# Projecting a memory's K and V straight into transposed form, on eight cores of one chip

## The chip, the cores and the metric

One Trainium2 chip, eight cores. Each core runs the same program on its own prompt sequence (2048 tokens) and its own 16 sample tokens. The metric is the device time of the slowest core, in microseconds (us).

Engine names in the profile: PE is TensorE (PEld its weight loads), DVE is VectorE, ACT is ScalarE, POOL is GpSimd, SP is SyncE, which here issues the loads of x and every store of an output. A PSUM bank is one of the eight buffers of 128 x 512 float32 (PS in the kernel) that its matmuls write to. Half clock means a stretch in which the profile's clock records grant TensorE 0.5 of its full speed. Filler is work that is queued in between other work, to be done where PE would otherwise wait.

## The reference, cut to what matters

```python
def mem_kv(mem, g_mem, w_kv):                       # once per layer
    kv = jnp.einsum('bnd,de->bne', rmsnorm(mem, g_mem), w_kv)
    k, v = jnp.split(kv, 2, axis=-1)                # both are outputs as well
    return k.reshape(b, n, 4, 256), v.reshape(b, n, 4, 256)

def mem_attend(u, k, v, w_q, w_o):
    q = einsum('btd,de->bte', u, w_q)               # heads of 256
    p = softmax(einsum('bthd,bnhd->bhtn', q, k) / 16)
    return einsum('btd,de->bte', einsum('bhtn,bnhd->bthd', p, v), w_o)
```

There are 256 memory tokens and 1024 channels, two layers, so four projections of 256 x 1024 by 1024 x 1024 per core. K and V have to be delivered (float32) and are used inside.

## The kernel before

The kernel doesn't attend with K and V as such. It folds K into the query weights (`wqk = wq . K^T`) and V into the output weights (`vwo = V . wo`), once per layer. Both folds, as the kernel writes them, take K and V with channels on the partitions. Before the change they were projected with tokens on the partitions, copied out, stored, and then turned by matmuls with an identity:

```python
# cut: indices, slices and views that don't matter here
def rows(name, od, nb, half):          # layer 0; 4 calls per tensor
    bk = nxt()                         # next PSUM bank
    for kc in range(NCH):              # 8 matmuls of 512 columns
        mm(PSv(bk, 0, 512), MEMN(kc, sl(nb*128, (nb+1)*128)), Wt(kc, hs), kc == 0, kc == NCH-1)
    cp(ST[i](), PSv(bk, 0, 512), eng=ACT)          # float32, for the store
    cp(NB(nb, hs), ST[i](), eng=DVE)               # bfloat16
    dma(SP, DV(od[0, nb*128:(nb+1)*128, hs]), ST[i](), f"rst{i}")

def turn(nb, half):                    # 4 calls per tensor
    for j in range(4):                 # 4 matmuls of 128 columns with the identity
        mm(PSv(bk, j*128, (j+1)*128), NB(nb, sl(c*128, (c+1)*128)), IDB(), True, True)
    cp(TR(...), PSr(bk, ...), eng=evac_eng())      # ScalarE and VectorE in turn

def foldk(dc):                         # 2 x 4 matmuls of 256 columns, 2 copies
    ...
```

These pieces are filler between other work. The parts of the schedule that matter here:

```python
# prelude: software pipeline over 16 blocks of x; step s does
#   stB(s-1): pool bands, stC(s-2): transposes of x block s-2, stA(s+1): statistics, then extra[s]
for i, a in enumerate(quad): extra[12 + i].append(lambda a=a: rows("wk0", mk_d, *a))
for i, a in enumerate(quad): extra[16 + i // 2].append(lambda a=a: turn(*a))
extra[11].append(lambda: norm_a(0, BUF[0], parts=2))    # ScalarE: squares, 2 x 1664 columns
extra[12].append(lambda: norm_r(0, BUF[0], RSTDE))      # PE: sums the squares, after rows(0)
for i in range(4):                                      # VectorE: 2 multiplications per step
    extra[13 + i].append(lambda i=i: norm_s(0, R_ATTN, BUF[0], RSTDE, cs=(2*i, 2*i+1)))
...
wq_turn(0)                             # turn wq, fold K: 8 x (8 matmuls of 128, 8 of 256)
for dc in range(NCH):
    if dc + 1 < NCH: wq_turn(dc + 1)
    foldk(dc)
    if dc == 0: samples_a()            # VectorE: 1.27 us multiplication, 0.68 us cast
# stC(15) ends with last_rows(): a 1.28 us VectorE multiplication, then the load of the V weights
late = rows(V) x4, turn(V) x4, foldv x8   # popped one or two per score chunk of the first two tiles
# layer 1: the same pieces, as fill in layer 0's MLP; the conv stage stands between that and layer 1's attention
```

The softmax here doesn't subtract the row's maximum and nothing guards it: scores larger than these inputs give would overflow.

## Time and profile before

| | before |
|---|---|
| time of the slowest core, median of the first 3 runs | 1623.22 us (1622.68 to 1623.79) |
| span of the profiled run, slowest core / fastest core | 1624.3 / 1618.2 us |
| PE, VectorE, ScalarE busy | 97%, 53%, 35% |

From the page of the kernel before, the busy time by engine (us, share of the span, instructions), and below it the shares of the chain of work that ended last:

```profile
PE 1575.0 (97%) x10104; PEld 906.3 (56%) x10104; DVE 854.2 (53%) x1907; ACT 560.8 (35%) x1054; POOL 113.9 (7%) x245
...
PE 92%; DVE 2%; ACT 2%; DMA 2%; issue 2%; POOL 0%; DVEq 0%; ACTq 0%; SPq 0%; POOLq 0%
```

PE is the bound, at 97% of the span and 92% of the chain, so I count work taken from VectorE (53%) or ScalarE (35%) only where PE waits for it. The groups of the kernel before by form show the matmuls concerned (line, engine, operation, out and in, shapes, count, then busy us, mean ns of one, idle us before them and what ended it). L292 is the line of the matmul helper:

```profile
L292 PE MATMUL PS<-MEM 128*128 128x512 bf16 x192 | 47.1, 383 | 0.0
...
L292 PE MATMUL PS<-MEM 128*128 128x256 bf16 x128 | 18.6, 294 | 2.1 <-DVE MEM L345 1.9 <-ACT MEM L343 0.2
...
L292 PE MATMUL PS<-MEM 128*128 128x128 bf16 x192 | 15.2, 227 | 1.2 <-DVE MEM L327 1.2
```

128 of the 192 matmuls of 512 columns are the projections and 64 of the 192 of 128 columns the transposes. The mean length of one record at 512 columns (383 ns) is more than the time from its start to the next one's start, so the records overlap. I take the time from start to start as a matmul's cost: in the traces 215.8 ns at 512 columns, 109.1 at 256, 55.8 at 128, at the full granted clock.

The waits view of the kernel before, PE alone, from 64 to 160 us (who waited for whom: us in total, times, longest):

```profile
PE PS L296 <- DVE MEM L339: 3.1, 1, 3.1
PE PS L292 <- DVE MEM L345: 2.7, 2, 1.9
PE PS L292 <- ACT MEM L343: 0.2, 1, 0.2
```

L345 is VectorE's copy, L343 ScalarE's. The 2.7 us are 1.87 us at the fold of K (ending at 93.6 us) and 0.84 us in the fold of V (about 149 us). The 3.1 us are the late x blocks at 64 us. VectorE is nearly full in the stretch of the K fold, as the windows view of the kernel before shows (busy us of each engine from 86 to 95 us, granted clock, DMA share, GB/s):

```profile
86.00:95.00 9.00, 6.94 (x90) 6.01 (x87) 8.33 (x14) 5.54 (x12) 0.90 (x1) 0.93 0.12 39
```

The engines stand in the order PE, PEld, DVE, ACT, POOL: VectorE is busy for 8.33 of 9 us on this core (5), and the granted clock was 0.93 in the mean.

### The profile page before, as it was taken

What the parts mean: (1) busy time and instruction counts of PE and PEld (TensorE: products, weight loads), DVE (VectorE), ACT (ScalarE), POOL (GpSimd) and SP (SyncE); (2) the same over time, 40 slices, a digit from 0 to 9 for tenths busy, and PEclk for the clock granted to TensorE, in tenths of its full rate; (3) what the DMA queues carried; (4) which work ended last, traced back from release to release, by engine and by line L of the source; (5) the groups of instructions that cost most, each with busy time, mean ns of one, the idle gap of its engine ahead of it and who ended that gap; (6) DMA issues with size and microseconds to landing.
All of it is one profiled execution on the core that took longest, in us unless ns stands there. A gap on an engine that the chain in (4) does not pass through costs nothing.

```text
span 1624.3 us, 28431 instructions; the slowest of 8 cores (1618.2 to 1624.3 us)
## 1 busy us (share of the span) xinstructions
PE 1575.0 (97%) x10104; PEld 906.3 (56%) x10104; DVE 854.2 (53%) x1907; ACT 560.8 (35%) x1054; POOL 113.9 (7%) x245
## 2 busy tenths in 40 slices
PE   4899999999999999999999999999999999999997
PEld 3775555555555556555555555555555555555565
DVE  5666675655444444445666665766455444442235
ACT  4756344541122222222133224433643112213453
POOL 2002121110000000000000001121010000000000
PEclk8899999999999999999999999999999999999999
DMA  9978793575537516066000009694654663000012
GB/s 228 208 116 156 161 183 68 122 148 77 85 66 126 107 24 105 1 104 109 1 1 1 1 1 151 130 201 96 126 118 68 101 105 52 14 1 1 40 64 108
DMA packets 84565, 145.13 MB, mean 89 GB/s; under 512 B 4286, under 2 KB 37310, under 8 KB 84412
## 3 DMA queue, kind: packets, MB, share of 16 engines
q0 software_dynamic: 67568, 84.08, 35.4%
q1 hardware_dynamic: 16860, 59.24, 10.6%
q8 instruction: 84, 1.38, 0.3%
q14 instruction: 53, 0.43, 0.1%
HBM read 212.42 MB, written 14.36 MB: 140 GB/s over the span
## 4 chain that ended last, share of the span: by engine, by line
PE 92%; DVE 2%; ACT 2%; DMA 2%; issue 2%; POOL 0%; DVEq 0%; ACTq 0%; SPq 0%; POOLq 0%
PE PS L292 89%; PE PS L296 2%; DVE MEM L327 1%; ACT MEM L319 1%; PE PS L301 1%; DMA MEM<-gv 1%; DMA MEM<-x 1%; ACT MEM L308 1%; DVE MEM L331 0%; DVE MEM L345 0%; DVE MEM L339 0%; POOL MEM L354 0%; ACT MEM L343 0%; DVEq L1389 0%; ACTq L1389 0%
## 5 line engine op out<-in xcount | busy, mean ns | idle before, releaser
L292 PE MATMUL PS<-MEM 128*128 128x416 bf16 (+7 forms) x9024 | 1501.3, 327 | 8.3 <-DVE MEM L345 2.7
L292 PEld LDWEIGHTS PS<-MEM 128*128 128x128 bf16 (+1 forms) x9024 | 837.3, 98 | 659.8 <-issue 38.5
L319 ACT ACTIVATE MEM<-PS 128x416 f32<-128x416 f32 (+5 forms) x469 | 238.9, 510 | 632.5 <-PE PS L292 622.7
L331 DVE TENSOR_TENSOR MEM<-PS,MEM 128x416 f32<-128x416 f32 (+6 forms) x533 | 297.8, 575 | 264.2 <-PE PS L292 256.1
L331 DVE TENSOR_TENSOR MEM<-MEM 128x416 bf16<-128x416 f32 (+3 forms) x282 | 159.9, 584 | 198.8 <-ACT MEM L319 189.5
L327 DVE SCALAR_TENSOR_TENSOR MEM<-MEM 128x416 bf16<-128x416 f32 (+7 forms) x322 | 176.9, 601 | 126.9 <-ACT MEM L319 108.5
L319 ACT ACTIVATE MEM<-MEM 128x416 bf16<-128x416 f32 (+9 forms) x299 | 185.2, 631 | 146.5 <-DVE MEM L331 111.6
L304 DVE SCALAR_TENSOR_TENSOR MEM<-MEM,PS 128x256 f32<-128x256 f32 x256 | 105.2, 420 | 72.0 <-PE PS L292 49.0
L343 ACT COPY MEM<-PS 128x512 f32<-128x512 f32 (+3 forms) x73 | 39.2, 536 | 129.5 <-PE PS L292 119.1
L296 PE MATMUL PS<-MEM 128*128 128x128 bf16 (+4 forms) x896 | 61.0, 248 | 16.3 <-DVE MEM L339 9.4
L296 PEld LDWEIGHTS PS<-MEM 128*128 128x128 bf16 (+2 forms) x896 | 49.2, 107 | 30.2 <-issue 28.6
L343 ACT CAST MEM<-PS 128x512 bf16<-128x512 f32 (+2 forms) x65 | 35.2, 554 | 68.0 <-PE PS L292 67.3
L345 DVE CAST MEM<-PS 128x512 bf16<-128x512 f32 (+1 forms) x76 | 48.5, 658 | 11.7 <-PE PS L292 11.7
L354 POOL DMA_DIRECT2D MEM<-cv x64 | 47.7, 745 | 13.4 <-PE PS L292 13.4
L319 ACT ACTIVATE PS<-PS 128x416 f32<-128x416 f32 (+3 forms) x67 | 33.2, 495 | 41.5 <-PE PS L292 41.1
L327 DVE SCALAR_TENSOR_TENSOR MEM<-PS,MEM 128x1024 f32<-128x1024 f32 (+1 forms) x17 | 21.8, 1283 | 44.1 <-ACT MEM L319 44.1
L301 PE MATMUL PS<-MEM 128*128 128x128 f32 (+5 forms) x184 | 25.0, 277 | 18.3 <-DMA MEM<-gv 8.4
L351 POOL MEMSET MEM<- 128x4 bf16 (+1 forms) x96 | 15.0, 159 | 359.1 <-PE PS L296 298.5
L301 PEld LDWEIGHTS PS<-MEM 128*128 128x128 f32 (+5 forms) x184 | 20.9, 146 | 21.4 <-issue 19.9
L339 DVE TENSOR_SCALAR MEM<-MEM 128x1024 bf16<-128x1024 f32 (+1 forms) x18 | 17.9, 997 | 24.0 <-ACT MEM L319 24.0
L354 POOL DMA_DIRECT2D MEM<-w_up x36 | 20.6, 582 | 132.5 <-PE PS L292 132.5
L354 POOL DMA_DIRECT2D MEM<-w_down x22 | 13.8, 635 | 202.2 <-PE PS L292 158.1
(28 smaller groups left out, 137.3 us busy)
## 6 DMA issues: line engine op xcount, KB each, us to landing
MEM<-ck SPq DMA_DIRECT2D x64, 512.0 KB, 6.2
MEM<-cv POOLq DMA_DIRECT2D x64, 256.0 KB, 5.8
MEM<-w_down POOLq DMA_DIRECT2D x6, 2048.0 KB, 17.7
MEM<-x SPq DMA_DIRECT2D x16, 512.0 KB, 14.2
MEM<-w_kv POOLq DMA_DIRECT2D x4, 2048.0 KB, 17.9
MEM<-w_o POOLq DMA_DIRECT2D x4, 2048.0 KB, 22.7
MEM<-w_up POOLq DMA_DIRECT2D x32, 256.0 KB, 13.0
MEM<-w_up POOLq DMA_DIRECT2D x4, 2048.0 KB, 17.1
```

The source lines that it names most:

```text
L292: P.add(PE, "c", lambda e, o=out.ap, l=lhsT.ap, r=rhs.ap: e.matmul(out=o, lhsT=l, rhs=r, start=start, stop=stop), [lhsT, rhs], [out])
L296: P.add(PE, "c", lambda e, o=out.ap, l=lhsT.ap, r=rhs.ap: e.matmul(out=o, lhsT=l, rhs=r, start=start, stop=stop, is_transpose=is_transpose ...
L301: P.add(PE, "c", lambda e, o=out.ap, i=in_.ap, d=ident.ap: e.transpose(out=o, in_=i, identity=d), [in_, ident], [out])
L304: P.add(DVE, "c", lambda e, o=out.ap, a=in0.ap, b=in1.ap, c=acc.ap: e.scalar_tensor_tensor(out=o, in0=a, scalar=1.0, in1=b, op0=ALU.mult, ...
L308: P.add(ACT, "c", lambda e, o=out.ap, i=in_.ap, a=acc.ap: e.activation(out=o, in_=i, func=AF.Square, accum_out=a), [in_], [out, acc])
L319: P.add(ACT, "c", lambda e, o=out.ap, i=in_.ap: e.activation(out=o, in_=i, func=func, bias=bias, scale=sc), rd, [out])
L327: P.add(eng, "c", lambda e, o=out.ap, a=in0.ap, b=in1.ap: e.scalar_tensor_tensor(out=o, in0=a, scalar=sc, in1=b, op0=op0, op1=op1), rd, [out])
L331: P.add(eng, "c", lambda e, o=out.ap, a=in0.ap, b=in1.ap: e.tensor_tensor(out=o, in0=a, in1=b, op=op), [in0, in1], [out])
L339: P.add(eng, "c", lambda e, o=out.ap, a=in0.ap: e.tensor_scalar(out=o, in0=a, scalar1=sc, scalar2=None, op0=op0), rd, [out])
L343: P.add(ACT, "c", lambda e, o=out.ap, i=in_.ap: e.copy(out=o, in_=i), [in_], [out])
L345: P.add(eng, "c", lambda e, o=out.ap, i=in_.ap: e.tensor_copy(out=o, in_=i), [in_], [out])
L354: return P.add(q, "d", lambda e, o=out.ap, i=in_.ap: e.dma_start(out=o, in_=i), [in_], [out], chan=chan, after=after)
```

## The change

Intent: swap the operands of the projection. Each matmul now loads a 128 x 128 block of the weights (LDWEIGHTS 128x128 in the trace) and takes the 256 normalised memory tokens as its 256 columns; K and V come out with channels on the partitions, as the folds take them. The transposes, their copies and a bfloat16 buffer go; the outputs are stored as [1024, 256] per layer, and the host lays them out (that time is not in the metric).

```diff
-    mk_d = dout("mk", [2, NMEM, D])            # mv alike
+    mk_d = dout("mk", [2, D, NMEM])
+    def project(Wt, memn, dst, st, od, k, chan):       # 4 calls per tensor
+        bk = nxt()
+        for j in range(2):
+            c = 2 * k + j
+            for kc in range(NCH):                      # 2 x 8 matmuls of 256 columns
+                mm(PSv(bk, j*NMEM, (j+1)*NMEM), Wt(kc, sl(c*128, (c+1)*128)), memn(kc), kc == 0, kc == NCH-1)
+        cp(st(), PSv(bk, 0, 2*NMEM), eng=ACT)
+        cp(dst, ..., eng=DVE)
+        dma(SP, DV(od[2*k*128:(2*k+2)*128, :].rearrange("(j p) n -> p j n", p=128)), ..., chan)
-        for i, a in enumerate(quad): extra[12 + i].append(lambda a=a: rows("wk0", mk_d, *a))
-        for i, a in enumerate(quad): extra[16 + i // 2].append(lambda a=a: turn(*a))
+        for k in range(4): extra[13 + k].append(lambda k=k: kv("wk0", mk_d, k))     # kv calls project
-        late.extend(rows("wv0") x4); late.extend(turn x4)
+        late.extend(kv("wv0") x4)
-                    for _ in range(1 if k == 0 or m > 3 else 2): late.pop(0)()
+                    late.pop(0)()
     # (rows and turn deleted in both layers, layer 1's fill list rebuilt with the same spacing,
     #  host: mk and mv transposed; all cut here)
```

Layer 0's K projections now stand at steps 13 to 16 of the prelude instead of 12 to 15.

More of the change, by code (lines that the diff above doesn't have):

```diff
@@ L165, in build_program @@
     ncp_d = dout("ncp", [2, D])
-    mk_d = dout("mk", [2, NMEM, D])
-    mv_d = dout("mv", [2, NMEM, D])
+    mk_d = dout("mk", [2, D, NMEM])
+    mv_d = dout("mv", [2, D, NMEM])
     nps_d = dout("nps", [NS, 15, D])
@@ L449, in build_program @@
     late = []
+    def project(Wt, memn, dst, st, od, k, chan):
[3 more added lines that the diff above has]
+            for kc in range(NCH):
+                mm(PSv(bk, j * NMEM, (j + 1) * NMEM), Wt(kc, sl(c * 128, (c + 1) * 128)), memn(kc), kc == 0, kc == NCH - 1)
+        cp(st(), PSv(bk, 0, 2 * NMEM), eng=ACT)
+        cp(dst, V(st.ap.rearrange("p (j n) -> p j n", j=2), st().ivs), eng=DVE)
+        dma(SP, DV(od[2 * k * 128:(2 * k + 2) * 128, :].rearrange("(j p) n -> p j n", p=128)),
+            V(st.ap.rearrange("p (j n) -> p j n", j=2), st().ivs), chan)
     def prelude():
@@ L454, in prelude @@
         MEMN = su.alloc(BF16, [NCH, NMEM])
-        NB = su.alloc(BF16, [2, D])
+        SQJ = su.alloc(BF16, [D])
         TR = su.alloc(BF16, [NCH, NMEM])
@@ L592, in mem_stats @@
             for nb in range(2):
-                sumsq(NB(nb), MR[nb](), st_(0, 16 + nb))
+                sumsq(SQJ(), MR[nb](), st_(0, 16 + nb))
                 rstd(16 + nb)
@@ L614, in prelude, with kv @@
         st_ctr = [0]
-        def rows(name, od, nb, half):
-            bk = nxt()
+        def kv(name, od, k):
             i = st_ctr[0] % 3
             st_ctr[0] += 1
-            hs = sl(half * 512, (half + 1) * 512)
-            Wt = W(name)
-            for kc in range(NCH):
-                mm(PSv(bk, 0, 512), MEMN(kc, sl(nb * 128, (nb + 1) * 128)), Wt(kc, hs), kc == 0, kc == NCH - 1)
-            cp(ST[i](), PSv(bk, 0, 512), eng=ACT)
-            cp(NB(nb, hs), ST[i](), eng=DVE)
-            dma(SP, DV(od[0, nb * 128:(nb + 1) * 128, hs]), ST[i](), f"rst{i}")
-        def turn(nb, half):
-            bk = nxt()
-            for j in range(4):
-                c = half * 4 + j
-                mm(PSv(bk, j * 128, (j + 1) * 128), NB(nb, sl(c * 128, (c + 1) * 128)), IDB(), True, True)
-            cp(TR(sl(half * 4, half * 4 + 4), sl(nb * 128, (nb + 1) * 128)), PSr(bk, "p (j t) -> p j t", j=4), eng=evac_eng())
+            project(W(name), MEMN, TR(sl(2 * k, 2 * k + 2)), ST[i], od[0], k, f"rst{i}")
         def wq_turn(dc):
@@ L695, in samples_c @@
             dma(POOL, SO(), DV(wsrc_sq(wsrc["wo0"])), f"w{slot_of['wo0']}")
-        quad = [(nb, half) for nb in range(2) for half in range(2)]
         extra = {s: [] for s in range(20)}
@@ L704, in prelude @@
         extra[7] = [poolws]
-        for i, a in enumerate(quad):
-            extra[12 + i].append(lambda a=a: rows("wk0", mk_d, *a))
-        for i, a in enumerate(quad):
-            extra[16 + i // 2].append(lambda a=a: turn(*a))
+        for k in range(4):
+            extra[13 + k].append(lambda k=k: kv("wk0", mk_d, k))
         extra[11].append(lambda: norm_a(0, BUF[0], parts=2))
@@ L735, in prelude @@
                 samples_c()
-        late.extend(lambda a=a: rows("wv0", mv_d, *a) for a in quad)
-        late.extend(lambda a=a: turn(*a) for a in quad)
+        late.extend(lambda k=k: kv("wv0", mv_d, k) for k in range(4))
         late.extend(lambda h=h, nb=nb: foldv(h, nb) for h in range(4) for nb in range(2))
@@ L758, in begin, with kv @@
             mem["n"] = s.alloc(BF16, [NCH, NMEM])
-            mem["st"] = [s.alloc(F32, [D]) for _ in range(2)]
-            mem["nb"] = s.alloc(BF16, [2, D])
+            mem["st"] = [s.alloc(F32, [512]) for _ in range(2)]
             n = mem["n"]
             dma(SP, V(n.ap.rearrange("p c n -> p (c n)"), n().ivs), DV(memn_d), "memn", after=tuple(spill))
-        def rows(name, od, nb, half):
-            bk = nxt()
-            st = mem["st"][nb]
-            hs = sl(half * 512, (half + 1) * 512)
-            Wt = W(name)
-            for kc in range(NCH):
-                mm(PSv(bk, 0, 512), mem["n"](kc, sl(nb * 128, (nb + 1) * 128)), Wt(kc, hs), kc == 0, kc == NCH - 1)
-            cp(st(hs), PSv(bk, 0, 512), eng=ACT)
-            cp(mem["nb"](nb, hs), st(hs), eng=DVE)
-            if half == 1:
-                dma(SP, DV(od[1, nb * 128:(nb + 1) * 128, :]), st(), f"kst{nb}")
-        def turn(dst, nb, half):
-            bk = nxt()
-            for j in range(4):
-                c = half * 4 + j
-                mm(PSv(bk, j * 128, (j + 1) * 128), mem["nb"](nb, sl(c * 128, (c + 1) * 128)), IDB(), True, True)
-            cp(dst[half](sl(0, 4), sl(nb * 128, (nb + 1) * 128)), PSr(bk, "p (j t) -> p j t", j=4), eng=evac_eng())
+        def kv(name, od, dst, k):
+            project(W(name), mem["n"], dst[k // 2](sl(k % 2 * 2, k % 2 * 2 + 2)), mem["st"][k % 2], od[1], k, f"kst{k % 2}")
         def foldk(dc):
@@ L807, in need_slot @@
             return fn
-        quad = [(nb, half) for nb in range(2) for half in range(2)]
         trk = [T(TRK.off + hf * 4 * NMEM * 2, BF16, [4, NMEM]) for hf in range(2)]
@@ L812, in kv1_fill @@
         items += [None] * 7
-        items += [lambda a=a: rows("wk1", mk_d, *a) for a in quad]
+        items += [lambda k=k: kv("wk1", mk_d, trk, k) for k in range(4)]
         items.append(lambda: swap("wk1", "wv1"))
-        items += [lambda a=a: turn(trk, *a) for a in quad]
+        items += [None] * 6
+        items += [lambda k=k: kv("wv1", mv_d, TRV, k) for k in range(4)]
+        items.append(lambda: swap("wv1", "wqT1"))
         items += [None] * 3
-        items += [lambda a=a: rows("wv1", mv_d, *a) for a in quad]
-        items.append(lambda: swap("wv1", "wqT1"))
-        items += [lambda a=a: turn(TRV, *a) for a in quad]
         def mid_k():
@@ L1186, in mid_s @@
                 if l == 0 and (k == 1 or k == 0 and m > 3):
-                    for _ in range(1 if k == 0 or m > 3 else 2):
-                        late.pop(0)()
+                    late.pop(0)()
                 if k == 0:
@@ L1488 @@
     new_conv_prompt = np.stack(g("ncp"), 0)[None]
-    mem_k_prompt = np.stack(g("mk"), 1).reshape(2, NCORES, NMEM, 4, 256)
-    mem_v_prompt = np.stack(g("mv"), 1).reshape(2, NCORES, NMEM, 4, 256)
+    mem_k_prompt = np.ascontiguousarray(np.stack(g("mk"), 1).transpose(0, 1, 3, 2)).reshape(2, NCORES, NMEM, 4, 256)
+    mem_v_prompt = np.ascontiguousarray(np.stack(g("mv"), 1).transpose(0, 1, 3, 2)).reshape(2, NCORES, NMEM, 4, 256)
     new_pool_sample = np.concatenate(g("nps"), 0)[None]
```

## The prediction

> **What bounds the kernel.** TensorE: busy 1575 of 1624.3 us (97%, the page's first part); the chain that ended last is 92% PE. VectorE is at 53%, ScalarE at 35%. Only PE time, or a wait of PE's, can shorten the run. PE's waits after 66 us are few (waits view): 0.19 and 1.87 us (ScalarE and VectorE copies) where layer 0's K is folded into wq, near 91 us; 0.84 us (VectorE copy) where V is folded into wo, near 148 us; and a few of about 1 us later, which the change doesn't touch.
>
> **What the change removes, adds and moves.** There are four projections (K, V in two layers). From start to start at the full granted clock a 512-column matmul takes 215.8 ns, a 256-column one 109.1, a 128-column one 55.8. [...]
> - Projection: 32 x 215.8 = 6.91 us becomes 64 x 109.1 = 6.98 us: +0.3 us for four. The 32 more weight loads are hidden: the folds' 256-column matmuls keep 109.1 ns with a new weight each.
> - Transposes: 4 x 16 x 55.8 ns = 3.6 us of PE gone.
> - Copies out of PSUM: 16 gone, 8 on ScalarE (584 ns), 8 on VectorE (684): 10 us, off the critical path except near 91 and 148 us. Each projection keeps its ScalarE copy (585) and VectorE cast (426).
> - Stores: the same bytes in 1 KB pieces instead of 2 or 4 KB. Today's land in 2.0 to 7.6 us; a staging buffer is reused 9 to 10 us later. I expect no wait.
> - Layer 0's K moves one step later in the prelude, and V folds come one per score chunk, not two.
>
> **On the critical path.** All PE work after 66 us: -3.3 us. Near 91 us VectorE has no slack (8.3 of 9 us busy, windows view): it loses two 0.68 us copies, gains a 0.43 us cast, and PE gets 0.86 us more work ahead of it (1.75 in, 0.89 out), so the wait should lose about 1.8 us. [...] core 5 runs at half clock for 6.8 us from 93.7 us, cores 1 and 7 not at all. From the load of wv to that of wo it is 14.9 us on cores 0, 3, 5 and 12.8 on core 1, so up to 2 us to gain on the slowest. Some comes back: warm core 1 has a further VectorE wait of 0.92 us; I take -1.2. The wait at 148 us: perhaps -0.6.
>
> Sum on a slow core: -3.3 - 1.8 - 1.2 - 0.6 = -6.9 us. Prediction 1616.3 us, range 1612 to 1620.5: 0.4% faster, "same" at 2%.
>
> **What would show it right.** On the helper's line, 128-column bf16 matmuls drop from 192 to 128, 512-column ones from 192 to 64, and 256-column ones rise from 128 to 384; PE busy about 3 us less; VectorE and ScalarE about 5 us less each; the 1.87 us wait gone or under 0.6 us; no half clock near 93 us.
>
> **What would make it wrong.** 256-column matmuls slower than 109 ns; ScalarE waiting for a staging buffer because 1 KB stores are slow; layer 0's V weights (landing 16 to 18.5 us after issue) needed before they land, since PE gets there some 5 us sooner; a clock drop elsewhere; a new wait on VectorE's cast. The matmul term alone gives 1619.9.
>
> Chances: faster by over 2% 0.01, within 2% 0.98, slower 0.01.

The three matmul times are those of the traces. The -1.2 us was an estimate from the traces (14.9 against 12.8 us from the load of wv to that of wo, less 0.92 us), and it assumed that the half clock goes when the wait goes, which was not shown. "Warm" core 1 is one that had the full granted clock at the folds.

## The result, and the profile after

| | before | after |
|---|---|---|
| median of 6 runs | 1623.82 us (1622.68 to 1625.79) | 1622.43 us (1621.63 to 1625.02) |
| ratio of fast runs | | 0.9992 (95%: 0.9979 to 1.0005) |
| repeated with the experiments, 5 rounds, median of the fast runs | 1624.31 us | 1621.51 us, ratio 0.9982 (0.9969 to 0.9995) |

A ratio is the mean time of one kernel's fast runs over that of the other's in the same rounds, so it is not quite the ratio of the medians. Executions in which one die ran at a lower clock are left out of the means. The change is worth 0.1 to 0.2% and counts as the same. The prediction was 0.4% (1616.3 us, at best 1612, at worst 1620.5), and the measured time lies above its range.

The slowest core's time is a blunt tool here. How long the loads at the start take differs from core to core by 2.5 to 5.5 us (the first transposing matmul of x block 10 starts between 61.9 and 65.4 us on the eight cores before, between 61.5 and 64.1 us after, between 60.5 and 65.9 us in a repeat of the changed kernel). So I also cut each core's trace at six PE instructions that all kernels share, and averaged the lengths over the eight cores. A is the first transposing matmul of x block 10 (step 12), B that of x block 15 (step 17), C the first score matmul of the attention, D the first value matmul of sample 0, E that of sample 8, F the first one of layer 1. These numbers are worked out from the start times in the traces:

| us, mean of 8 cores | A to B | B to C | C to D | D to E | E to F | F to end | A to end |
|---|---|---|---|---|---|---|---|
| before | 21.82 | 20.33 | 69.02 | 116.91 | 736.34 | 593.07 | 1557.49 |
| after | 23.33 | 18.82 | 68.31 | 116.91 | 735.00 | 593.16 | 1555.53 |
| after, repeated | 23.36 | 18.83 | 68.31 | 116.91 | 735.08 | 593.23 | 1555.72 |
| holds | K of layer 0 | K fold | V of layer 0 | | layer 1's K, V | | |

In all -1.96 us, of which layer 1 gave 1.34 and V of layer 0 0.71; 0.09 went back from F to the end. K of layer 0 gave nothing that can be told from zero: A to C is 42.15 us in both kernels. That it is the same to the hundredth is chance. A to C has a standard deviation of 1.2 to 1.3 us from core to core, and four executions whose program is the same up to C (after, its repeat, and e5 and e12 below) gave 42.12 to 42.40 us.

The busy time after, from the page, answers to that of before:

```profile
PE 1568.4 (97%) x10162; PEld 912.5 (56%) x10168; DVE 848.8 (52%) x1899; ACT 555.8 (34%) x1046; POOL 113.7 (7%) x245
...
PE 91%; DVE 2%; ACT 2%; DMA 2%; issue 2%; POOL 0%; DVEq 0%; ACTq 0%; SPq 0%; POOLq 0%
```

PE lost 6.6 us of busy time (the two lines are of different cores, with different time at half clock), VectorE 5.4 and ScalarE 5.0. The counts by form after are as planned (a few records of 512-column matmuls are missing from the trace, 58 of 64):

```profile
L292 PE MATMUL PS<-MEM 128*128 128x256 bf16 x384 | 47.3, 272 | 2.8 <-DVE MEM L345 2.7 <-ACT MEM L343 0.2
...
L292 PE MATMUL PS<-MEM 128*128 128x512 bf16 x58 | 15.5, 379 | 1.3 <-DVE MEM L345 0.9
...
L292 PE MATMUL PS<-MEM 128*128 128x128 bf16 x128 | 9.0, 219 | 1.2 <-DVE MEM L327 1.2
```

So the work left. The waits view after, PE alone, from 64 to 160 us, shows where the time went:

```profile
PE PS L292 <- DVE MEM L345: 3.6, 3, 1.8
PE PS L292 <- ACT MEM L319: 2.0, 2, 1.4
PE PS L292 <- ACT MEM L343: 0.2, 1, 0.2
```

The VectorE waits hardly shrank (1.75 us at the K fold, 0.93 us at the next fold, 0.94 us in the V fold). The second of them is not new: before, cores 1 and 7, which had the full clock at the K fold, waited 0.92 us there as well, and the six cores at half clock did not. PE at the K fold before, core 5, and after, core 4:

```profile
93.56 0.95 PE L292 MATMUL PS<-MEM 128*128 128x256 bf16 x4 [1.87 <-DVE MEM L345]
...
93.34 0.60 PE L292 MATMUL PS<-MEM 128*128 128x256 bf16 x4 [1.75 <-DVE MEM L345]
```

And there is a new line in the waits view: PE waits for ScalarE's L319, its activation helper. The timelines around it (start us, length us, engine, line, operation, out and in, shapes, count, then the idle time before and what ended it) show what that is. PE before, core 5:

```profile
68.30 4.02 PE L292 MATMUL PS<-MEM 128*128 128x512 bf16 x16
```

ScalarE before, the same core:

```profile
65.42 3.51 ACT L319 ACTIVATE MEM<-MEM 128x1 f32<-128x1 f32 x4
```

PE after, core 4:

```profile
67.45 0.86 PE L292 MATMUL PS<-MEM 128*128 128x416 bf16 x4 [1.41 <-ACT MEM L319]
68.93 1.26 PE L292 MATMUL PS<-MEM 128*128 128x416 bf16 x4 [0.62 <-ACT MEM L319]
```

ScalarE after, the same core:

```profile
65.28 3.51 ACT L319 ACTIVATE MEM<-MEM 128x1 f32<-128x1 f32 x4
```

ScalarE's 3.51 us are the two little rstd operations and the two squares of 1664 columns for the attention's norm (merged in this view under the first one's shape). Both kernels have them. Before, PE began the projection at 68.30 (8 of the 16 matmuls, merged with the norm's 8 under the projection's shape) while the squares were being made, and reached the norm's matmuls at 70.8, when the squares had been done since 68.9. (This core had also been held up by a late x block, the 3.1 us above.) After, the projection was one step later, and the norm's matmuls stood at the head of PE's queue: PE stopped for 1.41 and 0.62 us.

VectorE's timeline on the way to the K fold, before, core 5:

```profile
87.18 0.68 DVE L345 CAST MEM<-PS 128x512 bf16<-128x512 f32 x1
87.78 0.68 DVE L345 COPY MEM<-PS 128x512 f32<-128x512 f32 x1
88.38 0.68 DVE L345 CAST MEM<-PS 128x512 bf16<-128x512 f32 x1
88.98 1.20 DVE L327 SCALAR_TENSOR_TENSOR MEM<-MEM 128x416 bf16<-128x416 f32 x2
90.10 0.68 DVE L345 COPY MEM<-PS 128x512 f32<-128x512 f32 x1
90.82 1.28 DVE L327 SCALAR_TENSOR_TENSOR MEM<-MEM 32x1024 f32<-32x1024 f32 x1
92.13 1.89 DVE L345 CAST MEM<-PS 128x512 bf16<-128x512 f32 x3
```

And after, core 4:

```profile
86.82 0.68 DVE L345 COPY MEM<-PS 128x512 f32<-128x512 f32 x1
89.01 0.43 DVE L345 CAST MEM<-MEM 128x512 bf16<-128x512 f32 x1 [1.51 <-ACT MEM L343]
89.35 1.21 DVE L327 SCALAR_TENSOR_TENSOR MEM<-MEM 128x416 bf16<-128x416 f32 x2
90.47 0.68 DVE L345 COPY MEM<-PS 128x512 f32<-128x512 f32 x1
91.19 1.28 DVE L327 SCALAR_TENSOR_TENSOR MEM<-MEM 32x1024 f32<-32x1024 f32 x1
92.50 1.29 DVE L345 CAST MEM<-PS 128x512 bf16<-128x512 f32 x2
```

The two casts of the transposes (at 88.38, and one of the three at 92.13) are gone. In their place VectorE stands idle for 1.51 us: the cast of the last projection waits for ScalarE's copy, which waits for PE's 1.75 us of matmuls, and what is behind it in VectorE's queue waits too. The queue kept its order here: the two multiplications, which needed nothing that was new, began at 89.35 us, behind the cast at 89.01. The windows view after, core 5 again, from 86 to 95 us: VectorE has less to do (7.34 us), and the granted clock is full.

```profile
86.00:95.00 9.00, 7.09 (x88) 6.02 (x85) 7.34 (x11) 5.98 (x12) 0.90 (x1) 1.00 0.36 69
```

### The profile page after: what moved, and what is told of

It is laid out like the page before. It is cut to its first block, busy times and chain, and to the rows that moved or that the text cites. A ratio compares the mean times of both kernels' runs of the same rounds, so it can differ in the third digit from the quotient of the medians.

```text
span 1620.1 us, 28511 instructions; the slowest of 8 cores (1616.6 to 1620.1 us)
## 1 busy us (share of the span) xinstructions
PE 1568.4 (97%) x10162; PEld 912.5 (56%) x10168; DVE 848.8 (52%) x1899; ACT 555.8 (34%) x1046; POOL 113.7 (7%) x245
## 4 chain that ended last, share of the span: by engine, by line
PE 91%; DVE 2%; ACT 2%; DMA 2%; issue 2%; POOL 0%; DVEq 0%; ACTq 0%; SPq 0%; POOLq 0%
PE PS L292 88%; PE PS L296 2%; DVE MEM L327 2%; ACT MEM L319 1%; DMA MEM<-gv 1%; PE PS L301 1%; DMA MEM<-x 1%; ACT MEM L308 1%; DVE MEM L331 0%; DVE MEM L345 0%; DVE MEM L339 0%; ACT MEM L343 0%; POOL MEM L354 0%; DVEq L1362 0%; ACTq L1362 0%
## 5 line engine op out<-in xcount | busy, mean ns | idle before, releaser
L292 PE MATMUL PS<-MEM 128*128 128x416 bf16 (+5 forms) x9082 | 1495.1, 325 | 11.6 <-ACT MEM L319 3.9
L292 PEld LDWEIGHTS PS<-MEM 128*128 128x128 bf16 x9088 | 844.0, 98 | 650.6 <-issue 42.1
L319 ACT ACTIVATE MEM<-PS 128x416 f32<-128x416 f32 (+5 forms) x469 | 238.6, 510 | 650.1 <-PE PS L292 639.4
L331 DVE TENSOR_TENSOR MEM<-PS,MEM 128x416 f32<-128x416 f32 (+6 forms) x533 | 297.7, 574 | 264.7 <-PE PS L292 256.4
L331 DVE TENSOR_TENSOR MEM<-MEM 128x416 bf16<-128x416 f32 (+3 forms) x282 | 159.8, 583 | 196.9 <-ACT MEM L319 188.4
L319 ACT ACTIVATE MEM<-MEM 128x416 bf16<-128x416 f32 (+9 forms) x299 | 184.9, 630 | 147.7 <-DVE MEM L331 112.6
L345 DVE CAST MEM<-PS 128x512 bf16<-128x512 f32 (+1 forms) x68 | 43.0, 654 | 12.1 <-PE PS L292 12.1
L343 ACT CAST MEM<-PS 128x512 bf16<-128x512 f32 (+3 forms) x57 | 30.7, 548 | 48.7 <-PE PS L292 47.9
L319 ACT ACTIVATE PS<-PS 128x416 f32<-128x416 f32 (+3 forms) x67 | 33.1, 494 | 40.0 <-PE PS L292 39.6
```

The source lines that it names most:

```text
L292: P.add(PE, "c", lambda e, o=out.ap, l=lhsT.ap, r=rhs.ap: e.matmul(out=o, lhsT=l, rhs=r, start=start, stop=stop), [lhsT, rhs], [out])
L319: P.add(ACT, "c", lambda e, o=out.ap, i=in_.ap: e.activation(out=o, in_=i, func=func, bias=bias, scale=sc), rd, [out])
L331: P.add(eng, "c", lambda e, o=out.ap, a=in0.ap, b=in1.ap: e.tensor_tensor(out=o, in0=a, in1=b, op=op), [in0, in1], [out])
L343: P.add(ACT, "c", lambda e, o=out.ap, i=in_.ap: e.copy(out=o, in_=i), [in_], [out])
L345: P.add(eng, "c", lambda e, o=out.ap, i=in_.ap: e.tensor_copy(out=o, in_=i), [in_], [out])
```

## The experiments

All ran correctly on the chip. Theory A: the matmul term is right, and the layer 0 gain was lost to the moved projection (lost cover for ScalarE's squares) and to the order and amount of VectorE's work at the folds. Rivals: late x data or the clock; the transposed form itself (weight loads, 1 KB stores). Kernels e1 to e12 are single edits or named sets of them.

Summary (us, mean of 8 cores; in e11's profile die 0 ran at a lower clock, so its row is the four cores of its undisturbed die, for which the kernel before has 42.07, 69.02 and 736.34):

| | A to B | B to C | A to C | C to D | E to F | A to end |
|---|---|---|---|---|---|---|
| before | 21.82 | 20.33 | 42.15 | 69.02 | 736.34 | 1557.49 |
| after | 23.33 | 18.82 | 42.15 | 68.31 | 735.00 | 1555.53 |
| e1 K at steps 12 to 15 | 21.13 | 18.86 | 39.99 | 68.72 | 735.02 | 1553.81 |
| e2 norm ahead of the cast | 23.70 | 18.41 | 42.11 | 68.31 | 735.01 | 1555.53 |
| e3 last rows later | 22.42 | 19.47 | 41.89 | 68.54 | 735.01 | 1555.53 |
| e4 before, K later | 23.59 | 20.14 | 43.73 | 69.02 | 736.34 | 1559.49 |
| e5 V fold on ScalarE, banks | 22.99 | 19.41 | 42.40 | 67.21 | 735.32 | 1555.42 |
| e6 last rows on GpSimd | 23.28 | 18.04 | 41.32 | 68.31 | 735.29 | 1554.77 |
| e7 first combination | 21.25 | 25.96 | 47.21 | 67.21 | 734.95 | 1559.09 |
| e9 second combination | 21.45 | 19.85 | 41.30 | 67.31 | 734.82 | 1553.35 |
| e10 e1 and V fold on ScalarE | 21.04 | 19.01 | 40.05 | 67.21 | 735.09 | 1552.69 |
| e11 layer 1 alone (4 cores) | 22.15 | 20.55 | 42.70 | 69.02 | 734.94 | 1556.31 |
| e12 banks alone | 22.84 | 19.28 | 42.12 | 68.31 | 735.16 | 1555.49 |

In e1 four cores, and in e3 two, ran at about 0.81 of the clock for 4.7 to 4.9 us just after C (as I read the clock records of these two profiles), which is why their C to D is longer than 68.31 us; without it e1 would be about 0.4 us better.

### e1 and e4: is it the step?

e1 puts the projections of the changed kernel back:

```diff
-            extra[13 + k].append(lambda k=k: kv("wk0", mk_d, k))
+            extra[12 + k].append(lambda k=k: kv("wk0", mk_d, k))
```

> The changed kernel with layer 0's K projections put back at steps 12 to 15 of the prelude (as before the change), ahead of the sum of squares' matmul; nothing else. Theory A (cover): in the old order 1.7 us of projection in step 12 hid ScalarE's squares from PE; moving it one step later is what made the new PE waits of 0.3 to 2.3 us and 0.6 us before the first 416-column matmuls near 67 us. Then those waits fall to what they were before (none on six cores, one of 0.62 us on two), and the stretch from the transposes of x block 10 to the start of the attention falls from 42.15 us (mean of 8 cores, in both kernels) to about 40 us. Rival B (late x data or the clock): the waits near 67 us stay, on some cores, whatever the order of the projections. Under both the VectorE wait of 1.75 us at the fold of K stays near 1.7 us, since the queue of VectorE ahead of it is the same length when PE comes earlier.

e4 makes the same move in the kernel before, old form, transposes kept:

```diff
-            extra[12 + i].append(lambda a=a: rows("wk0", mk_d, *a))
+            extra[13 + i].append(lambda a=a: rows("wk0", mk_d, *a))
```

> The kernel before with one edit: layer 0's K projections at steps 13 to 16 instead of 12 to 15, in the old form, transposes kept. Theory A (the shift costs, not the transposed form): new PE waits of about 0.3 to 2.3 and 0.6 us before the first 416-column matmuls near 67 us, and the stretch from the transposes of x block 10 to the start of the attention grows from 42.15 to about 44 us. Rival B (it comes with the transposed form or from chance in the loads): no new wait, 42.1 us.

A to C came out at 39.99 us in e1 (about 40 was expected) and at 43.73 us in e4 (about 44). PE's timeline of e1, core 5, where the projection again runs up to the norm without a stop:

```profile
67.01 3.32 PE L292 MATMUL PS<-MEM 128*128 128x256 bf16 x24
```

And of e4, core 2, where the old form now has the wait:

```profile
66.62 0.86 PE L292 MATMUL PS<-MEM 128*128 128x416 bf16 x4 [1.90 <-ACT MEM L319]
68.11 1.54 PE L292 MATMUL PS<-MEM 128*128 128x416 bf16 x4 [0.62 <-ACT MEM L319]
```

The PE wait for the squares is 0.15 us in the mean of the cores before, 1.61 after, 0.38 in e1, 1.45 in e4. (e1 was not quite back to none on six cores, as expected: five cores kept 0.2 to 0.95 us.) The step costs, in either form; the transposed form is not at fault. How long PE waits still depends on when x arrives: in the changed kernel ScalarE, which had waited for a load of x, began the squares 1.0 us after A on core 3, where PE had no wait, and 2.6 us after A on core 5, where PE waited 2.9 us. But the rival, that the wait comes whatever the order, falls: over all the profiles its mean is 1.28 to 1.92 us in the eight with the late order and 0.15 to 0.61 us in the six with the early one. The wait is 1.2 to 1.3 us of the difference in both runs; in e1 the time at half clock between A and C fell as well (3.65 to 1.65 us), so not all of its 2.2 us is cover.

### e2, e3 and e6: what holds the K fold?

e2 puts the step's norm multiplications ahead of the projection in the order of `extra`, so that VectorE need not idle:

```diff
-        for k in range(4): extra[13 + k].append(lambda k=k: kv("wk0", mk_d, k))
         for i in range(4): extra[13 + i].append(lambda i=i: norm_s(...))
+        for k in range(4): extra[13 + k].append(lambda k=k: kv("wk0", mk_d, k))
```

> The changed kernel, K projections still at steps 13 to 16, but within a step VectorE's norm multiplications are queued ahead of the projection's cast. Theory A (order on VectorE): in the changed kernel VectorE stands idle 1.5 us at about 87.5 us, since the cast of the last projection, which must wait for PE and ScalarE, is ahead of norm multiplications (1.21 us) that wait for nothing; so the two copies taken away bought idle time, not an earlier end. Then the PE wait at the fold of K falls from 1.75 to about 0.5 us. Rival B (VectorE's amount of work, or what stands behind the norm, sets the wait): it stays within 0.3 us of 1.75. The waits near 67 us stay (0.3 to 2.3 us).

e3 moves VectorE's 1.28 us multiplication behind the first fold; e6 gives it to GpSimd:

```diff
-            if tb == 15: last_rows(); dma(POOL, SV(), ...)      # e3: in stC
+            if dc == 0: last_rows(); dma(POOL, SV(), ...)       # e3: after foldk(0)
```

```diff
-            stt(UF(p=pr), XB[...](p=pr), st_(2, tb, pr), GBC(p=pr), ALU.mult, ALU.mult)   # e6
+            tsc(UF(p=pr), XB[...](p=pr), st_(2, tb, pr), ALU.mult, eng=POOL)
+            tt(UF(p=pr), UF(p=pr), GBC(p=pr), ALU.mult, eng=POOL)
```

> The changed kernel with the 1.28 us VectorE multiplication for the last pool rows (and the load of the V weights that waits for it) put behind the first fold of K. If the PE wait of 1.75 us at the fold is VectorE's queue, it falls by about 1.28 us to 0.5 us; the next VectorE wait (0.92 us, at the second fold) may grow by up to 1.3 us as the work comes there. If the wait is of something else (ScalarE's copy, the weights), it stays at 1.75. The V weights come 1 to 2 us later and are still in time.

> The changed kernel with the last pool rows' 1.28 us VectorE multiplication done on GpSimd (two operations). The earlier run that only put it behind the first fold kept the sum of the two VectorE waits at the folds at 2.68 us (0.32 + 2.36). Theory (the sum is VectorE's amount of work behind the last x block): the sum falls by about 1.28 us to 1.4 us. Rival (the waits are latency of single copies, not amount): the sum stays above 2.2 us. The V weights' load waits for GpSimd's two operations, so it may start 2 to 3 us later; still in time.

PE's waits for VectorE at the first and second fold (us, cores at full clock):

| | first | second | sum |
|---|---|---|---|
| after | 1.75 | 0.93 | 2.68 |
| e2 | 1.34 | 0.92 | 2.26 |
| e3 | 0.32 | 2.36 | 2.68 |
| e6 | 0.26 | 1.59 | 1.85 |

PE in e6, core 4, and VectorE in e2, core 4:

```profile
90.10 0.60 PE L292 MATMUL PS<-MEM 128*128 128x256 bf16 x4 [0.26 <-DVE MEM L345]
95.18 6.01 PE L292 MATMUL PS<-MEM 128*128 128x256 bf16 x71 [1.59 <-DVE MEM L345]
...
90.22 0.43 DVE L345 CAST MEM<-MEM 128x512 bf16<-128x512 f32 x1 [0.72 <-ACT MEM L343]
91.20 0.69 DVE L345 COPY MEM<-PS 128x512 f32<-128x512 f32 x1 [0.56 <-PE PS L296]
```

e2 gave 0.4 us where I expected 1.25: so neither statement about it held. The idle time was split rather than filled: 0.72 us ahead of the cast, and 0.56 us ahead of x block 15's copy, on which VectorE can't start until PE has done its transposes. It then has 0.68 + 1.28 + 0.68 us to do before the second half of the first fold, while PE has only about 1.3 us of other work. e3 moved the 1.28 us and the sum stayed 2.68: moving the work inside VectorE's queue moved the wait. e6 took the work away and the sum fell by 0.83, not 1.28, to a value between the theory's 1.4 and the rival's 2.2; VectorE now waited 0.69 us for ScalarE's statistics of the sample rows ahead of the second fold's cast, which may be where the rest went. So the waits at the folds come in part from VectorE's amount of work behind the last x block (0.83 of 2.68 us) and in part from its order (0.42); the rest was not taken apart. The prediction had counted PE's extra 0.86 us as cover for VectorE; but that PE work lies ahead of the very matmuls that VectorE's queue waits for, so it delays both.

### e5 and e12: the V fold, and the last 0.3 us of layer 1

e5 sends all copies of layer 0's V fold to ScalarE, and skips eight numbers of the PSUM bank counter in layer 1's fill; e12 has the bank edit alone.

```diff
-                cp(W("vwo0")(...), PSv(bk, 0, 512), eng=evac_eng())
+                cp(W("vwo0")(...), PSv(bk, 0, 512), eng=ACT)          # e5
         def mid_k():
+            bank_ctr[0] += 8                                          # e5, e12
```

> The changed kernel with two edits that are read in different stretches. First, all copies of layer 0's V fold go to ScalarE. Theory: the PE wait of 0.94 us near 146 us comes from a copy that stands on VectorE behind the eight norm multiplications (about 0.65 us each) of the third score tile, so spreading the folds could not help; then the wait falls under 0.3 us and the stretch from the start of the attention to the first sample's value matmuls falls from 68.31 to about 67.4 us. Rival (too few PSUM banks in any case, or ScalarE can't carry it): it stays or moves to ScalarE. Second, 8 numbers of the PSUM bank counter are skipped in layer 1's fill, so that at the conv stage it stands where it stood before the change. Theory: the 0.28 us that layer 1 lost of its 1.63 us (waits of 1.13 instead of 0.97 us, and one of 0.12) is the ring of banks, one bank shorter where it goes from 7 to 8; then the stretch from sample 8 to layer 1's first sample falls from 735.0 to about 734.7 us. Rival (order of copies on VectorE): 735.0.

> The changed kernel with only the PSUM bank counter skipped by 8 in layer 1's fill, so that the ring stands at the conv stage as before the change (the earlier run of this edit had a second edit upstream, and gave 735.32 us instead of the 734.7 expected). Theory (one bank less between use and reuse where the ring goes from 7 to 8): the stretch from sample 8 to layer 1's first sample falls from 735.0 to about 734.7 us, the conv-stage waits to about 0.97 us each. Rival (the waits there follow from how VectorE's and ScalarE's queues happen to stand, which every edit upstream shifts): 735.0 or above.

The V fold's wait of 0.94 us was gone on every core, and C to D fell from 68.31 to 67.21 us, of which 0.28 came back in D to E. The first theory holds: one VectorE copy stood behind eight norm multiplications, and spreading the folds over more chunks did not help that. The bank theory falls: E to F was 735.32 and 735.16 us, not 734.7, and the two waits at the conv stage in e12 were 1.00 and 1.20 us (after: 1.00 and 1.13; before: 1.00 and 0.97). Every edit upstream moved these two waits a little (E to F between 734.82 and 735.32 in all runs of the new form); what sets them is left open.

### e11: layer 1 alone

Layer 0 as before the change, layer 1 in the new form.

```diff
         # (in outline, against the kernel before) prelude and late list: rows and turn, as before the change
         items += [lambda k=k: kv("wk1", mk_d, trk, k) for k in range(4)]     # layer 1 as changed
```

> Only layer 1's K and V in the transposed form; layer 0 as before the change. Theory: layer 1, in the stretch where PE never waits, yields the matmul term (1.63 us less a 0.3 us wait at the conv stage), and layer 0's K yields nothing, its 0.8 us going to the lost cover. Then the stretch from sample 8 to layer 1's first sample is about 735.0 us as in the changed kernel (736.34 before), the stretch from x block 10 to the attention stays 42.15 us and that to the first sample's value matmuls 69.02 us as before; after x block 10 in all some 1556.2 us on the mean of 8 cores. Rival (the loss is spread, layer 1's stores in 1 KB pieces cost there too): layer 1's stretch falls by under 1 us.

Its profiled execution is counted as fast, but die 0 ran at a clock of 0.981 and took 1633.8 us, against 0.993 and 1620.5 us on die 1, so only die 1 is used. Layer 1's stretch is 734.94 us there, 1.40 us under the kernel before, with C to D unchanged; the rival falls. A to C is 42.70 instead of the expected 42.15 us, two of the four cores having run at half clock for 6.8 us near 93 us. The time in five rounds was inconclusive (ratio 1.001, 0.998 to 1.005); it includes that execution of 1638.5 us, and the other five had a mean of 1623.8 us against 1624.6 us before.

### e7, e9, e10: does it add up?

e7 joins e1, e5, e6 and also gives the sample rows' norm to GpSimd and its cast to ScalarE. e8 is the changed kernel unedited in the same rounds (its figures stand with the result above).

```diff
-            stt(XSR(p=P16), XSR(p=P16), st_(2, 18, P16), GBC(p=P16), ALU.mult, ALU.mult)
-            cp(UCB(p=P16), XSR(p=P16))
+            tsc(XSR(p=P16), XSR(p=P16), st_(2, 18, P16), ALU.mult, eng=POOL)
+            tt(XSR(p=P16), XSR(p=P16), GBC(p=P16), ALU.mult, eng=POOL)
+            cp(UCB(p=P16), XSR(p=P16), eng=ACT)
```

> The changed kernel with everything that the runs point to: K projections at steps 12 to 15; last pool rows and the sample rows' norm on GpSimd, the sample rows' cast on ScalarE; copies of layer 0's V fold on ScalarE; the bank counter as before the change at the conv stage. If the single effects add up: 1.7 us (cover) + 1.3 to 2.2 us (VectorE work) + 0.9 us (V fold) + 0.3 us (banks) under the changed kernel on the stretch that follows x block 10, so about 1551 us there instead of 1555.5; the time 4 to 5 us under the changed kernel's, near 1618 us, 0.3 to 0.4% under the kernel before, still same at 2%.

> The changed kernel unedited, timed in the same rounds. By the profile of all eight cores the change is worth 1.96 us after x block 10 (1557.49 to 1555.53), so a ratio near 0.9988; the prediction's 0.9957 would need 5 us more.

e7 was slower than the changed kernel: 1626.74 us (median of its fast runs), ratio to the kernel before 1.0011 (0.9997 to 1.0026). ScalarE's timeline, core 5:

```profile
97.63 1.04 ACT L343 CAST MEM<-MEM 16x1024 bf16<-16x1024 f32 x1 [5.64 <-POOL MEM L331]
```

And PE's, the same core:

```profile
99.29 1.97 PE L292 MATMUL PS<-MEM 128*128 128x256 bf16 x9 [6.65 <-ACT MEM L343]
```

GpSimd took 2.83 and 2.33 us for what took VectorE 1.27 us; ScalarE's cast waited for that, the fold's copies stood behind the cast, and PE stopped for 6.65 us. It is the change's own lesson at four times the size. (GpSimd's two operations were one by a per-row scalar and one of two tensors, on 16 x 1024 float32. In the changed kernel its two-tensor operation on 128 x 1024, L331, float32 in and bfloat16 out, took 2.35 us, so fewer partitions were not faster here.)

e9 queues that cast just ahead of its use, and drops the bank edit:

```diff
         def samples_b():
+            cp(UCB(p=P16), XSR(p=P16), eng=ACT)
-            if dc == 3: samples_b()      # and samples_c at 5
+            if dc == 5: samples_b()      # and samples_c at 7
```

> The changed kernel with K projections at steps 12 to 15, the last pool rows on GpSimd, all copies of layer 0's V fold on ScalarE, and the sample rows' norm on GpSimd; against the earlier combination, the ScalarE cast that reads GpSimd's result is queued only right ahead of the matmuls that need it, and these come two folds later. The earlier combination lost 6.65 us to PE waiting for a ScalarE copy that stood behind that cast, which waited for GpSimd's 2.84 and 2.33 us operations. If that was all, the wait falls under 1 us, the sum of PE waits between 87 and 100 us under 1.2 us, and the stretch after x block 10 is about 1551 us instead of 1555.5 (mean of 8 cores); ratio to the kernel before about 0.995 to 0.996. If the order of queues is at fault elsewhere too (ScalarE waits again), it stays above 1553.

e10 is e1 and the V fold copies on ScalarE, nothing else.

> The changed kernel with only the two edits that worked by themselves: K projections at steps 12 to 15, and all copies of layer 0's V fold on ScalarE. The gains add: 1.7 us and 0.8 to 1.1 us under the changed kernel on the stretch after x block 10, so about 1552.8 us; ratio to the kernel before about 0.9970, against 0.998 to 0.999 for the changed kernel.

| 5 rounds | median of the fast runs | ratio to the kernel before (95%) |
|---|---|---|
| before | 1624.59 us | |
| e9 | 1620.19 us | 0.9973 (0.9959 to 0.9986) |
| e10 | 1620.02 us | 0.9971 (0.9958 to 0.9985) |

e10 landed where the sum of the single effects put it (1552.8 us expected after A, 1552.69 measured; one core's D to E is 1.8 us longer because of a half-clock stretch at 273.6 us). e9 did not: 1553.35 us, not 1551. It is rid of the waits at the folds, but a new 1.28 us wait for ScalarE's cast stands at the sample matmuls and one of 0.7 to 1.7 us for a VectorE copy ahead of the folds, and all eight cores ran at half clock for 3.4 us soon after the former. e10 is the simpler of the two: 0.3% under the kernel before, clear of zero; the changed kernel has 0.1 to 0.2%, clear of zero in one of its two sets of runs. No pair of these was timed closely enough to say by time alone that e10 beats the changed kernel; the traces do (1552.69 and 1555.5 to 1555.7 us after A).

## Why the prediction was wrong, point by point

The sum was -6.9 us on a slow core. Term by term (mean of 8 cores, from the traces):

| step of the prediction | predicted | measured |
|---|---|---|
| 256-column matmuls at 109.1 ns, transposes gone: -3.3 us | -3.3 | right: -3.3 |
| wait at the K fold loses 1.8 us | -1.8 | -0.15 (both folds, cores at full clock: 2.98 to 2.83) |
| half clock near 93 us goes away, less the second fold's wait | -1.2 | -0.9 |
| V fold's wait | -0.6 | +0.10 (0.84 to 0.94) |
| K one step later: no cost given | 0 | +1.46 (0.15 to 1.61) |
| half clock near 67 us: not foreseen | 0 | +0.4 (2.45 to 3.23 us of it from A to B; 2.45 in the repeat) |
| waits at the conv stage: not foreseen | 0 | +0.29 |

These rows add up to -2.1 us, and to -2.0 with the 0.09 us from F to the end, against -1.96 us measured. The rows for the K fold and its clock come from B to C: it took 19.36 us before on the two cores at full clock, and 20.33 in the mean of eight; 18.76 after at full clock, and 18.82 in the mean. At full clock it fell by 0.60 us, of which 0.45 are the two calls of transposes that lay there and 0.15 the wait. The clock's share of the mean fell from 0.97 to 0.06 us.

- **The matmul term was right.** In the new kernel the 256-column matmuls run at 109.1 to 109.2 ns from start to start, with a new weight load each. The same matmul after layer 1's fill comes 1.63 us earlier after E (518.43 to 516.80 us, core 5); for two projections, 2 x (64 x 109.1 - 32 x 215.8 - 16 x 55.8) ns gives -1.63. C to D gives the same for V of layer 0 (-0.71, with the term at -0.81 and the wait 0.10 longer).
- **The clock term came out near its size, and that was luck.** I had tied the half clock near 93 us to the wait at the fold. That wait stayed (1.75 us), and yet the half clock near there was gone on seven of eight cores, in the profile and in its repeat. In e5 and e12, whose program is the same up to C, four and five of the eight cores had it again. That is 11 of 32 cores in the new form, against six of eight before (and three of four on e11's undisturbed die): less often, but not gone, and what sets it stays open. The length of PE's gaps alone doesn't tell: gaps of 0.19 and 1.87 us before were followed by half clock on six of eight cores (3.4 us on three, 6.8 us on three) and not on two; in e6 no core had it at the folds, with gaps of 0.26 and 1.59 us; in e9 all eight had 3.4 us of it after a gap of 1.28 us. It also costs less than it looks: a core of the changed kernel with 3.4 us of half clock took 19.3 us from B to C against 18.76, only 0.5 us more, since it then lacked the second fold's wait of 0.93 us.
- **The step that failed first: "it loses two 0.68 us copies, gains a 0.43 us cast, and PE gets 0.86 us more work ahead of it, so the wait should lose about 1.8 us."** VectorE's busy time there did fall, but the wait only went from 1.87 to 1.75 us. I counted lengths and not the order: the new cast waits for PE through ScalarE, VectorE idled 1.51 us in front of it, and PE's extra work delays VectorE's queue too. e2, e3 and e6 show that both the order and the amount of VectorE's work bear on the wait.
- **The step that failed second: "Layer 0's K moves one step later in the prelude", listed without a cost.** The projection in step 12 was doing a second job: it covered ScalarE's squares. The move cost 1.46 us of PE waits and, with the half clock near 67 us (0.4), ate what the matmuls (0.8), the clock near 93 us (0.9) and the fold's wait (0.15) gave between A and C. e1 and e4 show it from both sides: -2.2 us in A to C when undone, +1.6 us when done alone.
- **The V fold's wait: "perhaps -0.6".** It needed another engine for the copy (e5, gone), not more even spacing.
- **What I feared and did not happen:** the 1 KB stores landed in 2.2 to 10.4 us (K) and 2.1 to 8.0 us (V), medians 3.6 and 3.3, against medians of 4.1 and 3.0 before, and no engine waited for a staging buffer in the views read. The V weights landed 14.5 to 19.1 us after issue on the eight cores and were in time: PE waited for no DMA between 64 and 160 us.
- **The time itself.** -1.4 us in the first six runs and -2.8 us in the repeat (medians) bracket the -1.8 to -2.0 us of the traces; the start of the program differs by more than that between cores.

## What to carry to other kernels

Before moving a piece of filler work, ask what it was covering: look at which engine's result the next instruction in the queue needs, and when that is ready without the filler. When a copy is taken from a full engine, look at what its queue will wait for next: here one dependent cast left VectorE idle for 1.51 us where work had been saved, and work moved within the queue moved the wait (e3: 2.68 us in sum before and after). For effects of a few us in 1600, cut the traces at instructions that both kernels share and average over the cores; the slowest core's time varies with how the first loads arrive (A by 2.5 to 5.5 us here).
